# A fourth seven in the first column pair of w_down's second half, sevens loaded by rows, and tile 1's banks opened one column pair sooner

## The chip, the core and the metric

The kernel runs on one core of one Trainium2 chip. The time is device microseconds of one execution; three runs gave 1061.6, 1061.85 and 1062.74, the median is 1061.85 us. Nothing else runs on the chip.

The engines are named as in the profile: PE (TensorE; PEld is its weight load), DVE (VectorE), ACT (ScalarE), POOL (GpSimd) and SP, whose queue starts nearly all transfers.

## The reference, cut to what matters

One layer of a hybrid decoder in float32 for 256 positions of 2048 channels: an attention sub-layer, then a channel mixer. The change is in the mixer's last product:

```
h = rmsnorm(x, pre_ffn_g[l])
u = causal_dwconv(h @ w_up[l], conv_w[l], conv_b[l])
gate, val = jnp.split(u, 2, axis=-1)
y = (jax.nn.gelu(gate, approximate=True) * val) @ w_down[l]
x = x + rmsnorm(y, post_ffn_g[l])
```

`w_up` is 2048 x 11264, `w_down` is 5632 x 2048.

## The kernel before

**Three passes.** Each float32 operand is split into a high part (fp32r, a cast on ACT) and a low part (the rest, a subtraction on DVE), and a product is three matmuls: high by high, high by low, low by high. `split` (L286) and `w_split` (L107, its cast is L118 and its subtraction L121) do that; `products` (L973, matmul L975) issues the three. Weights come in units of 512 KB through five buffers `raw`, split into five pairs of buffers `whi` and `wlo`.

**The mixer in halves.** The 5632 rows of `w_down` are taken in two halves of 22 blocks of 128 rows. For each half the up-projection makes the 22 activation blocks `G` (positions are two tiles of 128, t = 0 and 1), and then `w_down` is applied to them in two column pairs, n = 0 and n = 2, of twice 512 columns. The first half leaves its sums in `y_sb`, the second adds to them. While the up-projection runs, DVE, ACT and POOL also make, for the first few pairs of blocks, four sums of quarters of `G` (L943 to L954), held split in `sums`.

**Fours and sevens.** A unit is two blocks of 128 rows and 512 columns. `four` (L1024) multiplies it plainly: 2 blocks by 2 tiles are 4 products, 12 matmuls, into two banks. A round is one `four` for each half of the column pair, 24 matmuls. `seven` (L988) does the work of one round, 2 blocks by 2 tiles by 2 column halves, with 7 products instead of 8 (21 matmuls, the Strassen-Winograd scheme): it takes sums of the weight blocks (four subtractions on DVE, L1002 to L1005, written in place into `raw`) and the sums of `G`. Three of its products are issued at once, on bank a (`w11`), b (`w21`) and e (`w22`); the other four, into banks d, f, c and g, come after the round's fours, from the function `others` that it returns. `SEVENS` lists in which rounds of a column pair a seven stands ahead of the fours. After the last seven `fold` (L1031) adds the four shared banks a, c, d and f into `y_sb`, in the second half with eight additions on DVE and a copy on ACT. At the end of a column pair `down` (L963) adds banks b, g, e and h to `y_sb` (L965), which frees them for the next pair; in the second half it also takes the squares (L967) and multiplies by the gain.

**Banks.** PSUM has eight banks here, four tagged `acc` and four tagged `att`, given out in turn: a new one waits until the oldest free one has been read for the last time.

**The last 512 columns.** In the second half the second pair (`tail`) does only the columns of n = 2. The last 512 columns are done after it: tile 0 in bank e, tile 1 in two banks `b1` of 256 columns each, so that half of tile 1 can be finished while PE does the other (L1140 on). `b1` is opened by a matmul with `start` (L1113) that only marks the banks as written, and then ACT copies tile 1's sums of the first half into them (L1114), so that the matmuls of `mm3` (L284) add to these.

**Order.** PE's order is the program's. DVE, ACT, POOL and SP are put in order by a scheduler when the program is built, except in a few stretches; the change is in scheduled ones. SP also brings back the residual, `x_end` (L1131, two loads of 1 MB), into the memory of `sums`, so it waits until the last seven is done.

Of the kernel before, what the change touches and what calls it, by code (L numbers as in the profile page):

```python
# [17 lines left out]
P = 128  # L18
# [6 lines left out]
NEG = -1e30  # L25
FHALF = 22
HOLD = 6
SEVENS = (((0, 1, 3, 4), (0, 1, 3, 4)), ((0, 2, 4), ()))
LOW = (14, 4, 4, 4)
ROOM = 112  # L30

# [2 lines left out]
def hybrid_layer(ctx: ExitStack, tc: tile.TileContext, x, pre_mix_g, w_in, b_forget, sinks,  # L34
# [3 lines left out]
    pe, act, dve, pool, sp = nc.tensor, nc.scalar, nc.vector, nc.gpsimd, nc.sync  # L38
    xf, of = x[0], out[0]
    w_in, w_out, w_up, w_down = w_in[0], w_out[0], w_up[0], w_down[0]  # L40
# [11 lines left out]
    def bank(tag="acc"):  # L52
        return ps.tile([P, 512], F32, tag=tag, bufs=4, name="bank_" + tag)
# [13 lines left out]
    UNIT = 1024  # L67
    WB = 5

    def w_load(src, a, c, pin=False):  # L70
        raw = wp.tile([P, UNIT], F32, tag="raw", bufs=5, name="raw")
        i = sp.dma_start(raw[:, :a * c].rearrange("p (a c) -> p a c", a=a), src)
        if pin:
            tc.keep_in_program_order(i)
        return raw, a, c
# [3 lines left out]
    def w_parts(n, keep=None, held=True):  # L79

        if keep and keep[0] is None:
            return keep[1]
        where, pre, nb = (keep[0], "h", keep[1]) if keep else (wp, "w", WB)
        hi = where.tile([P, UNIT], F32R, tag=pre + "hi", bufs=nb, name="whi")
        if where is not wp:
            lo = where.tile([P, UNIT], F32R, tag=pre + "lo", bufs=nb, name="wlo")
            return hi[:, :n], lo[:, :n]
        lo = where.tile([P, UNIT + 128], F32R, tag=pre + "lo", bufs=nb, name="wlo")
        at = 0
        if held:  # L90
            at = LOW[unit[0] % period[0]] * 4
            unit[0] += 1
        return hi[:, :n], lo[:, at:at + n]
# [35 lines left out]
    def w_rows(w, k0, a, c0, c):  # L129
        return w[k0 * P:(k0 + a) * P, c0:c0 + c].rearrange("(a p) c -> p a c", p=P)  # L130
# [18 lines left out]
    for i in range(2):  # L149
        cs = slice(i * 256, (i + 1) * 256)  # L150
# [135 lines left out]
    def split(hi, lo, src):  # L286
        act.copy(hi, src)  # L287
        dve.tensor_tensor(lo, src, hi.bitcast(F32), op=ALU.subtract)  # L288

    with tc.tile_pool(name="mixp", bufs=1) as mp:  # L290
# [3 lines left out]
        att = tc.tile_pool(name="att", bufs=1)  # L294
# [114 lines left out]
        halves = slice(0, 64), slice(64, 128)  # L409
# [192 lines left out]
        for p0, npair, cols in ((0, 3, 384), (3, 3, 384), (6, 2, 272)):  # L602
# [3 lines left out]
            for k0 in range(0, KT, per):  # L606
                na = min(per, KT - k0)
                hi, lo = w_unit(w_rows(w_in, k0, na, c0, cols), na, cols)
# [211 lines left out]
    with tc.tile_pool(name="ffn", bufs=1) as fp:  # L820
# [87 lines left out]
        for half in range(2):  # L908
# [70 lines left out]
            def parts_of(k, t):  # L979
                return G[k][:, t * P:(t + 1) * P], G[k][:, 256 + t * P:256 + (t + 1) * P]  # L980

            def split_512(dst, i, src):
                cs = slice(i * 512, i * 512 + 512)
                hi, lo = dst[0][:, cs], dst[1][:, cs]
                split(hi, lo, src)
                return hi, lo

            def seven(n, u, last, banks, opened):  # L988

                b, e, g, a, c, d, f = banks  # L990
                k = half * FHALF + u * 2
                left, right = [w_load(w_rows(w_down, k, 2, m * 512, 512), 2, 512)[0]
                               for m in (n, n + 1)]
                b11, b21, b12, b22 = (x[:, i * 512:i * 512 + 512] for x in (left, right)
                                      for i in range(2))
                s1, s2, s3, s4 = [(sums[:, u, i * P:i * P + P],
                                   sums[:, u, 512 + i * P:640 + i * P]) for i in range(4)]
                dst = w_parts(UNIT, held=False)
                w11 = split_512(dst, 0, b11)
                w22 = split_512(dst, 1, b22)  # L1000
                w21 = split_512(w_parts(UNIT, held=False), 0, b21)
                dve.tensor_tensor(b11, b12, b11, op=ALU.subtract)  # L1002
                dve.tensor_tensor(b12, b22, b12, op=ALU.subtract)
                dve.tensor_tensor(b22, b22, b11, op=ALU.subtract)
                dve.tensor_tensor(b21, b21, b22, op=ALU.subtract)  # L1005
                products(a, parts_of(u * 2, 0), *w11, opened, last)
                products(b, parts_of(u * 2 + 1, 0), *w21, opened)
                products(e, s4, *w22, opened)

                def others():  # L1010
                    dst = w_parts(UNIT, held=False)
                    t1 = split_512(dst, 0, b11)
                    t3 = split_512(dst, 1, b12)
                    dst = w_parts(UNIT, held=False)
                    t2 = split_512(dst, 0, b22)
                    t4 = split_512(dst, 1, b21)
                    products(d, s1, *t1, opened, last)
                    products(f, s3, *t3, opened, last)
                    products(c, s2, *t2, opened, last)
                    products(g, parts_of(u * 2 + 1, 1), *t4, opened)  # L1020

                return others
# [30 lines left out]
            for n in (0, 2):  # L1053
                opened = []
                tail = half and n
                at = SEVENS[half][n // 2]
                shared = [bank("att") for _ in range(4 if at else 0)]
                b, e, g = [bank() for _ in range(3)]
                h = None if tail else bank()
                for i in range(FHALF // 2 - len(at)):  # L1060
                    others = None
                    if i in at:
                        u = at.index(i)
                        others = seven(n, u, u == len(at) - 1, (b, e, g, *shared), opened)
                    four(n, len(at) + i, (b, g), opened)
                    if not tail:
                        four(n + 1, len(at) + i, (e, h), opened)
                    if others:
                        others()
                    if at and i == at[-1]:  # L1070
                        fold(n, *shared)
                    if i == max((0, *at)):
                        for args, kw in gains:
                            pool.tensor_tensor(*args, **kw)
                later_on = None if tail else lambda *args, **kw: gains.append((args, kw))
                for t, x in enumerate((b, g)):
                    down(t, n, x, later_on)
                if not tail:
                    for t, x in enumerate((e, h)):
                        down(t, n + 1, x, later_on)  # L1080
# [27 lines left out]
            q.dma_start(of[t * P:(t + 1) * P, cs], y_sb[:, t, cs])  # L1108

        held = []  # L1110
        b1 = [bank("att"), bank("att")]
        for x, cs in zip(b1, halves):
            pe.matmul(x[:, cs], G[0][:, 0:P], G[0][:, 0:256], start=True, stop=False)  # L1113
            act.copy(x[:, cs], y_sb[:, 1, 1536:2048][:, cs])  # L1114
        for u in range(len(at), FHALF // 2):
            hi, lo = w_unit(w_rows(w_down, FHALF + u * 2, 2, 1536, 512), 2, 512,
                            keep=(None, [rest[:, c:c + 2, :].rearrange("p a c -> p (a c)")
# [10 lines left out]
                    held.append(args)  # L1128
        x_sb = main.tile([P, 2, D], F32, tag="x", name="x_end")
        for t in range(2):  # L1130
            sp.dma_start(x_sb[:, t, :], x_dram[t * P:(t + 1) * P, :])  # L1131
        ctx.enter_context(tc.manual_schedule(
            engines={mybir.EngineType.Activation, mybir.EngineType.DVE, mybir.EngineType.Pool,
                     mybir.EngineType.SP}))
# [47 lines left out]
```

## Time and profile before

| | us |
|---|---|
| median of three runs | 1061.85 |
| the profiled execution | 1063.41 |
| its span, first to last instruction | 1061.7 |
| PE busy | 1050.2 (99%) |
| DVE busy | 803.8 (76%) |
| ACT busy | 634.0 (60%) |
| POOL busy | 252.1 (24%) |
| granted clock of PE, mean | 0.999 |

The first half's `w_down` lies between about 577 and 692 us, the second half's first column pair between 932.8 and 990.6, its second up to 1020.7, the last 512 columns up to 1053.7. A profiled row gives the start and the length of an instruction, in brackets how long its engine had been idle and what ended that. Rows with "x2" hold two instructions in a row. A matmul's length is from its start to the modelled end of its output, and the next one starts before that, so the price of one is the distance of two starts.

### The profile page before, as it was taken

The page shows a single profiled execution, that of the slowest core. Times are in us where ns is not written, and L with a number is a line of the kernel's source. Part 1 is how long each engine was busy: PE and PEld are TensorE (multiplying, and loading weights), DVE is VectorE, ACT ScalarE, POOL GpSimd, SP SyncE. Part 2 cuts the span into 40 slices and gives each one's busy share as a digit, 9 for nine tenths or more (in the row PEclk, how much of TensorE's full clock was granted, in tenths as well). Part 3 has the DMA queues.
Part 4 walks back from the last instruction along what each step waited for, and adds up shares of the span by engine and source line. Part 5 has one row for each costly group of instructions (what it writes and reads, how often), then busy time and mean ns, then how long its engine had stood idle before and what let it go on. Part 6 is the DMA issues. An engine that isn't in the chain of part 4 may idle for free.

```text
span 1061.7 us, 16409 instructions
## 1 busy us (share of the span) xinstructions
PE 1050.2 (99%) x5941; PEld 914.6 (86%) x5941; DVE 803.8 (76%) x1330; ACT 634.0 (60%) x1119; POOL 252.1 (24%) x278
## 2 busy tenths in 40 slices
PE   9999999999999999999999999999999999999996
PEld 7889988888889888888888888888888888888886
DVE  5989877876468787777768888868786777787653
ACT  6767766677557666655556555556565556555450
POOL 4253235441122433312111000013321212100210
PEclk9999999999999999999999999999999999999999
DMA  8645665555875766666664666866576656557742
GB/s 279 204 120 169 179 204 189 180 158 160 297 237 178 226 201 197 200 189 201 185 195 139 209 207 196 251 194 192 179 211 192 193 181 199 175 162 267 270 154 80
DMA packets 165550, 207.10 MB, mean 195 GB/s; under 512 B 6844, under 2 KB 131036, under 8 KB 164444
## 3 DMA queue, kind: packets, MB, share of 16 engines
q1 hardware_dynamic: 165148, 205.65, 61.9%
q8 instruction: 47, 0.77, 0.3%
q10 hardware_dynamic: 320, 0.40, 0.1%
q14 instruction: 35, 0.29, 0.1%
HBM read 201.68 MB, written 4.21 MB: 194 GB/s over the span
## 4 chain that ended last, share of the span: by engine, by line
PE 90%; DVE 4%; DMA 2%; issue 2%; ACT 1%; POOL 0%; SPq 0%; DVEq 0%; POOLq 0%; ACTq 0%
PE bank_acc L262 21%; PE bank_att L262 15%; PE bank_acc L975 13%; PE bank_acc L284 13%; PE bank_acc L269 11%; PE bank_att L269 8%; DMA raw<-in_w_down_dram 2%; PE bank_att L975 2%; DVE wlo L121 1%; PE bank_att L450 1%; PE bank_att L485 1%; PE bank_att L494 1%; DVE wlo L288 1%; PE bank_att L225 1%; PE bank_acc L881 1%
## 5 line engine op out<-in xcount | busy, mean ns | idle before, releaser
L121 DVE TENSOR_TENSOR wlo<-raw,whi 128x1024 fp32r<-128x1024 f32 (+3 forms) x335 | 408.7, 1233 | 140.4 <-ACT whi L118 133.5
L118 ACT CAST whi<-raw 128x1024 fp32r<-128x1024 f32 (+3 forms) x334 | 340.8, 1035 | 196.7 <-issue 90.7
L262 PE MATMUL bank_acc<-hT,whi 128*128 128x512 f32 x1024 | 245.6, 392 | 0.0
L262 PEld LDWEIGHTS bank_acc<-hT,whi 128*128 128x128 f32 x1024 | 188.2, 188 | 37.1
L857 POOL TENSOR_TENSOR u<-u,rowf 128x256 f32<-128x256 f32 x88 | 94.5, 1095 | 447.3 <-DVE u L856 444.3
L975 PE MATMUL bank_acc<-whi,G 128*128 128x512 f32 x520 | 167.6, 389 | 0.1
L262 PE MATMUL bank_att<-hT,whi 128*128 128x512 f32 x704 | 165.7, 390 | 0.0
L262 PEld LDWEIGHTS bank_att<-hT,whi 128*128 128x128 f32 x704 | 130.6, 188 | 26.2
L269 PEld LDWEIGHTS bank_acc<-hT,wlo 128*128 128x128 f32 x1024 | 123.5, 188 | 3.2
L269 PE MATMUL bank_acc<-hT,wlo 128*128 128x256 f32 x1024 | 125.8, 278 | 0.0
L975 PEld LDWEIGHTS bank_acc<-whi,G 128*128 128x128 f32 x520 | 97.6, 188 | 20.3 <-DVE y_sb L965 0.5
L975 PE MATMUL bank_acc<-wlo,G 128*128 128x512 f32 x260 | 101.2, 389 | 0.0
L269 PEld LDWEIGHTS bank_att<-hT,wlo 128*128 128x128 f32 x704 | 83.6, 188 | 1.9
L269 PE MATMUL bank_att<-hT,wlo 128*128 128x256 f32 x704 | 83.9, 277 | 0.0
L284 PE MATMUL bank_acc<-whi,oT 128*128 128x512 f32 (+1 forms) x272 | 81.8, 379 | 0.0
L287 ACT CAST whi<-raw 128x512 fp32r<-128x512 f32 x77 | 44.4, 621 | 27.2 <-DMA raw<-in_w_down_dram 14.5
L288 DVE TENSOR_TENSOR wlo<-raw,whi 128x512 fp32r<-128x512 f32 x77 | 52.7, 727 | 9.9 <-ACT whi L287 9.8
L284 PEld LDWEIGHTS bank_acc<-whi,oT 128*128 128x128 f32 x272 | 50.2, 188 | 9.3
L975 PEld LDWEIGHTS bank_acc<-wlo,G 128*128 128x128 f32 x260 | 48.8, 188 | 9.8
L284 PE MATMUL bank_acc<-wlo,oT 128*128 128x512 f32 (+1 forms) x136 | 51.2, 377 | 0.0
L284 PE MATMUL bank_acc<-whi,hT 128*128 128x384 f32 (+1 forms) x192 | 46.9, 323 | 0.0
L859 ACT ACTIVATE yg<-u,cw 128x256 f32<-128x256 f32 x44 | 26.5, 603 | 33.7 <-POOL u L857 33.7
(250 smaller groups left out, 1284.4 us busy)
## 6 DMA issues: line engine op xcount, KB each, us to landing
raw<-in_w_up_dram SPq DMA_DIRECT2D x176, 512.0 KB, 4.5
raw<-in_w_down_dram SPq DMA_DIRECT2D x88, 512.0 KB, 4.9
raw<-in_w_in_dram SPq DMA_DIRECT2D x51, 512.0 KB, 4.9
raw<-in_w_out_dram SPq DMA_DIRECT2D x32, 512.0 KB, 4.7
raw<-in_w_in_dram SPq DMA_DIRECT2D x16, 384.0 KB, 3.3
cb<-c_dram SPq DMA_DIRECT2D x8, 256.0 KB, 4.2
x_sb<-in_x_dram SPq DMA_DIRECT2D x2, 1024.0 KB, 6.0
x_dram<-x_sb SPq DMA_DIRECT2D x2, 1024.0 KB, 5.9
```

The source lines that it names most:

```text
L118: i1 = act.copy(hi[:, cs], raw[:, cs])
L121: i2 = dve.tensor_tensor(lo[:, cs], raw[:, cs], hi[:, cs].bitcast(F32), op=ALU.subtract)
L225: pe.matmul(b, hi[:, a, m * P:(m + 1) * P], hT[:, kt, 0:512], start=(kt == 0), stop=(kt == KT - 1))
L262: pe.matmul(b, hi[:, a, m * P:(m + 1) * P], hT[:, kt, 0:512], start=(kt == 0), stop=(last == (0, kt)))
L269: pe.matmul(b[:, 256:512], lo[:, a, m * P:(m + 1) * P], hT[:, u * 4 + a, 0:256], start=False, stop=(last == (1, u * 4 + a)))
L284: pe.matmul(b, a, r[:, cols], start=(first and i == 0), stop=(last and i == 2))
L287: act.copy(hi, src)
L288: dve.tensor_tensor(lo, src, hi.bitcast(F32), op=ALU.subtract)
L450: pe.matmul(sb[e][:, cs], a[r, t * P:(t + 1) * P], b[r, 0:nk], start=(n == 0), stop=(n == 2))
L857: pool.tensor_tensor(u[:, 2:258], u[:, 2:258], rowf, op=ALU.mult)
L859: act.activation(y, u[:, 2:258], AF.Identity, bias=cw[:, 3, ch:ch + 1], scale=cw[:, 2, ch:ch + 1])
L975: pe.matmul(b, x, r, start=b not in opened and not i, stop=closes and i == 2)
```

## The change

Three things are changed.

1. `SEVENS` gives the second half's first column pair sevens in rounds 0, 1, 3 and 4 instead of 0, 2 and 4. The pair has 7 rounds of fours then instead of 8. `most` becomes 4, so the up-projection of that half makes a fourth set of sums.
2. A seven's weights, a square of two blocks by two column halves, are loaded as two rows of 1024 columns (`top`, `low`) instead of as two columns of two blocks (`left`, `right`), and split with `split_into` in four pieces (512, 1024, 1024 and 1024 wide) instead of seven of 512.
3. The two matmuls and two copies that open `b1` move from behind the tail pair to behind its first round.

A fourth edit, which keeps the loads of `x_end` in program order, is made only if `at` is not empty there; it is empty here, so nothing follows from it.

```diff
-SEVENS = (((0, 1, 3, 4), (0, 1, 3, 4)), ((0, 2, 4), ()))
+SEVENS = (((0, 1, 3, 4), (0, 1, 3, 4)), ((0, 1, 3, 4), ()))
...
-            def split_512(dst, i, src):
-                cs = slice(i * 512, i * 512 + 512)
-                hi, lo = dst[0][:, cs], dst[1][:, cs]
-                split(hi, lo, src)
-                return hi, lo
+            def split_into(dst, src, n):
+                hi, lo = (x[:, :n * 512] for x in dst)
+                split(hi, lo, src[:, :n * 512])
+                return [(hi[:, i:i + 512], lo[:, i:i + 512]) for i in range(0, n * 512, 512)]
...
-                left, right = [w_load(w_rows(w_down, k, 2, m * 512, 512), 2, 512)[0]
-                               for m in (n, n + 1)]
-                b11, b21, b12, b22 = (x[:, i * 512:i * 512 + 512] for x in (left, right)
-                                      for i in range(2))
+                top, low = [w_load(w_rows(w_down, k + i, 1, n * 512, 1024), 1, 1024)[0]
+                            for i in range(2)]
+                b11, b12, b21, b22 = (x[:, i:i + 512] for x in (top, low) for i in (0, 512))
...
-                dst = w_parts(UNIT, held=False)
-                w11 = split_512(dst, 0, b11)
-                w22 = split_512(dst, 1, b22)
-                w21 = split_512(w_parts(UNIT, held=False), 0, b21)
+                (w11,) = split_into(w_parts(UNIT, held=False), top, 1)
+                w21, w22 = split_into(w_parts(UNIT, held=False), low, 2)
...
-                    dst = w_parts(UNIT, held=False)
-                    t1 = split_512(dst, 0, b11)
-                    t3 = split_512(dst, 1, b12)
-                    dst = w_parts(UNIT, held=False)
-                    t2 = split_512(dst, 0, b22)
-                    t4 = split_512(dst, 1, b21)
+                    t1, t3 = split_into(w_parts(UNIT, held=False), top, 2)
+                    t4, t2 = split_into(w_parts(UNIT, held=False), low, 2)
...
                     if i == max((0, *at)):
                         for args, kw in gains:
                             pool.tensor_tensor(*args, **kw)
+                    if tail and i == (at[-1] + 4 if at else 0):
+                        b1 = [bank("att"), bank("att")]
+                        for x, cs in zip(b1, halves):
+                            pe.matmul(x[:, cs], G[0][:, 0:P], G[0][:, 0:256], start=True,
+                                      stop=False)
+                            act.copy(x[:, cs], y_sb[:, 1, 1536:2048][:, cs])
...
         held = []
-        b1 = [bank("att"), bank("att")]
-        for x, cs in zip(b1, halves):
-            pe.matmul(x[:, cs], G[0][:, 0:P], G[0][:, 0:256], start=True, stop=False)
-            act.copy(x[:, cs], y_sb[:, 1, 1536:2048][:, cs])
...
-            sp.dma_start(x_sb[:, t, :], x_dram[t * P:(t + 1) * P, :])
+            i = sp.dma_start(x_sb[:, t, :], x_dram[t * P:(t + 1) * P, :])
+            if at:
+                tc.keep_in_program_order(i)
```

The change takes lines away and puts others in, so the line numbers of what lies behind differ: the fold's additions L1044 to L1051 are L1036 to L1043 after it, the opening L1113 is L1070; L965 and L121 keep theirs.

Where it moves instructions, the built programs show it. On DVE, at the end of the second half's first column pair, the order before is this. The banks `acc` 9938, 9940, 9939 and 9941 are b, g, e and h; L121 is the split of a unit, L1049 to L1051 the end of the fold.

```order
L121 TENSOR_TENSOR wlo_10378<-raw_10375,whi_10377 128x1024
L1049 TENSOR_TENSOR y_sb_3952<-y_sb_3952,s_10275 128x512
L1050 TENSOR_TENSOR s_10275<-bank_att_9936,s_10275 128x512
L121 TENSOR_TENSOR wlo_10407<-raw_10404,whi_10406 128x1024
L1051 TENSOR_TENSOR y_sb_3952<-y_sb_3952,s_10275 128x512
L121 TENSOR_TENSOR wlo_10429<-raw_10426,whi_10428 128x1024
L121 TENSOR_TENSOR wlo_10447<-raw_10444,whi_10446 128x1024
L965 TENSOR_TENSOR y_sb_3952<-bank_acc_9938,y_sb_3952 128x512
L965 TENSOR_TENSOR y_sb_3952<-bank_acc_9940,y_sb_3952 128x512
L121 TENSOR_TENSOR wlo_10465<-raw_10462,whi_10464 128x1024
L965 TENSOR_TENSOR y_sb_3952<-bank_acc_9939,y_sb_3952 128x512
L965 TENSOR_TENSOR y_sb_3952<-bank_acc_9941,y_sb_3952 128x512
```

On DVE at the same place after the change, where banks b, g, e and h are 9897, 9899, 9898 and 9900:

```order
L121 TENSOR_TENSOR wlo_10385<-raw_10382,whi_10384 128x1024
L1041 TENSOR_TENSOR y_sb_3952<-y_sb_3952,s_10261 128x512
L1042 TENSOR_TENSOR s_10261<-bank_att_9895,s_10261 128x512
L121 TENSOR_TENSOR wlo_10403<-raw_10400,whi_10402 128x1024
L1043 TENSOR_TENSOR y_sb_3952<-y_sb_3952,s_10261 128x512
L965 TENSOR_TENSOR y_sb_3952<-bank_acc_9897,y_sb_3952 128x512
L965 TENSOR_TENSOR y_sb_3952<-bank_acc_9899,y_sb_3952 128x512
L121 TENSOR_TENSOR wlo_10421<-raw_10418,whi_10420 128x1024
L965 TENSOR_TENSOR y_sb_3952<-bank_acc_9898,y_sb_3952 128x512
L965 TENSOR_TENSOR y_sb_3952<-bank_acc_9900,y_sb_3952 128x512
```

Before, two splits of units stood between the end of the fold and the four L965; now the first two L965 follow the fold at once, and one split, that of the eighth unit after the last seven, stands ahead of the third. On PE, the third of these banks (e, read by the third L965) is the one that the next column pair's second product is given.

On PE, before, the opening of `b1` (banks `att` 10612 and 10613) stands between the tail pair's last products and the last 512 columns; `acc` 10402 is bank e of tile 0:

```order
L975 MATMUL bank_acc_10403<-wlo_10591,G21_7488 128x512
L975 MATMUL bank_acc_10403<-whi_10590,G21_7488 128x512
L1113 MATMUL bank_att_10612<-G0_7467 128x256
L1113 MATMUL bank_att_10613<-G0_7467 128x256
L975 MATMUL bank_acc_10402<-whi_10620,G0_7467 128x512
L975 MATMUL bank_acc_10402<-wlo_10621,G0_7467 128x512
L975 MATMUL bank_acc_10402<-whi_10620,G0_7467 128x512
L284 MATMUL bank_att_10612<-whi_10620,G0_7467 128x256
```

On PE after the change, the opening (banks 10376 and 10377) stands between the tail pair's first and second unit:

```order
L975 MATMUL bank_acc_10353<-wlo_10357,G1_7420 128x512
L975 MATMUL bank_acc_10353<-whi_10356,G1_7420 128x512
L1070 MATMUL bank_att_10376<-G0_7419 128x256
L1070 MATMUL bank_att_10377<-G0_7419 128x256
L975 MATMUL bank_acc_10351<-whi_10384,G2_7421 128x512
L975 MATMUL bank_acc_10351<-wlo_10385,G2_7421 128x512
```

The pair of opening matmuls has moved ten units ahead; the matmul that first adds to `b1` (L284) stands where it stood.

## The prediction

> **What bounds the kernel now.** I read the page first, then the chain of waits from 940 us on, then what TensorE (PE) waited for, then the timeline at the places that the change touches.
>
> ```profile
> span 1061.7 us, 16409 instructions
> PE 1050.2 (99%) x5941; PEld 914.6 (86%) x5941; DVE 803.8 (76%) x1330; ACT 634.0 (60%) x1119; POOL 252.1 (24%) x278
> ```
>
> PE is busy for 1050.2 of 1061.7 us, so the number of products sets the time, and what else there is to gain lies in the few places where PE stands still. The chain from 940 us on (start, length, what) shows one of them:
>
> ```profile
> 971.71 2.04 PE bank_att L975 x9
> 973.75 46.93 PE bank_acc L975 x207
> 1020.68 0.02 issue
> 1020.70 0.84 ACT whi L118
> ...
> 1023.30 0.28 ACT bank_att L1114
> 1023.58 0.04 issue
> 1023.62 0.62 PE bank_att L284 x3
> ...
> 1024.94 0.71 PE bank_att L284 x6
> ```
>
> From 973.75 us on, 207 matmuls follow each other without a break: 46.93 / 207 = 0.2267 us each, which is the price of a 512-wide matmul here (its own row says 0.39, because neighbours overlap). Then the chain leaves PE for ScalarE (ACT) until 1023.62. These are all the waits of PE for such work (total us, times, longest), and its weight loads (PEld) tell the same:
>
> ```profile
> PE bank_att L284 <- ACT bank_att L1114: 1.4, 2, 1.1
> PEld bank_att L284 <- ACT bank_att L1114: 2.0, 2, 1.5
> PEld bank_acc L975 <- DVE y_sb L965: 0.5, 1, 0.5
> ```
>
> The first two lines are the opening of tile 1's banks. The third is a column pair's start that waits for VectorE (DVE) to empty a bank. No row names a weight split or a weight load: the feeding of the sevens is hidden, and a cheaper feeding gains nothing by itself.
>
> **The change part by part.**
>
> *The fourth seven.* The pair had 3 sevens of 21 matmuls and 8 rounds of 24 (63 + 192 = 255); it gets 4 and 7 (84 + 168 = 252). Three matmuls at 0.2267 us go: -0.68 us. They lie in a stretch without a break, so all of it counts. Bounds: none worth the name.
>
> It also needs one more set of sums. DVE and ACT rows of these, and GpSimd's (POOL) four small operations before them:
>
> ```profile
> L948 POOL TENSOR_TENSOR s<-yv x7: 2319/2322/2381, 365.1 to 763.6; 128x128 f32<-128x128 f32 x7
> L287 ACT CAST sums<-s x7: 621/622/625, 369.0 to 767.4; 128x512 fp32r<-128x512 f32 x7
> L288 DVE TENSOR_TENSOR sums<-s,sums x7: 691/693/693, 369.7 to 768.1; 128x512 fp32r<-128x512 f32 x7
> ```
>
> Seven such sets were made beside the up-projection, four of them in the first half, and PE's waits above name none. The eighth is put at nothing; were its cover gone, 0.62 + 0.69 = 1.3 us would show.
>
> *Tile 1's banks.* PE's starts around the opening:
>
> ```profile
> 1021.21 0.39 PE L975 MATMUL bank_acc<-whi,G 128*128 128x512 f32 x1
> 1022.70 0.38 PE L284 MATMUL bank_att<-whi,G 128*128 128x256 f32 x1 [1.10 <-ACT bank_att L1114]
> ...
> 1023.62 0.39 PE L284 MATMUL bank_att<-whi,G 128*128 128x256 f32 x1 [0.31 <-ACT bank_att L1114]
> ...
> 1024.08 0.40 PE L975 MATMUL bank_acc<-whi,G 128*128 128x512 f32 x1
> ```
>
> From 1021.21 to 1024.08 are 2.87 us, for one 512-wide matmul (0.23) and six 256-wide ones (0.71, the chain's last row above): 1.93 us are lost. ACT filled the banks behind a weight cast and the squares of the pair just finished. With the opening after the pair's first unit, the copies have ten units of 2.72 us (12 x 0.2267) to run in. On PE the two opening matmuls cost the same there and wait for banks that the first steps of the fold have long given back; on ACT the copies stand between weight casts that run several units ahead, and hold up nobody. What is late next at the old place? Nothing that a row names: no PE wait is for a split. So -1.93 us; the least that the rows allow is the 1.4 us put down as idle.
>
> *Sevens by rows.* Each of the now 12 sevens makes four splits instead of seven, with the same elements. Two 512-wide splits, queued, take 1.20 us (966.47 to 967.67 below), a 1024-wide one 1.14 (976.50 to 977.64), so DVE saves some 0.2 us a seven, off the path. Whether longer rows arrive sooner is bounded by the issue rows (median us to landing):
>
> ```profile
> raw<-in_w_up_dram SPq DMA_DIRECT2D x176, 512.0 KB, 4.5
> raw<-in_w_down_dram SPq DMA_DIRECT2D x88, 512.0 KB, 4.9
> ```
>
> w_up comes in pieces of 1 KB, w_down of 2 KB, and the longer pieces are not the quicker: nothing for the step to 4 KB. The first half holds one wait that this could move, the third PE wait above, worth 0.33 us (worked below): bounds -0.33 and +0.33, and I take 0.
>
> *The wait that the change adds.* After the last seven DVE has the fold (L1044 to L1051), then four adds L965 that empty the pair's banks. Number the units of four after the last seven 1, 2, 3 and so on: the pair used to end after unit 6, now it ends after unit 4, 24 matmuls or 5.44 us sooner, while the fold is as long as before. The next pair's third bank is free only after the third L965, and in the new order the splits of units 4 to 8 stand ahead of that. On DVE, ACT and SP's queue, before:
>
> ```profile
> 966.47 1.29 DVE L288 TENSOR_TENSOR wlo<-raw,whi 128x512 fp32r<-128x512 f32 x2
> 967.67 0.68 DVE L1044 TENSOR_TENSOR y_sb<-bank_att,y_sb 128x512 f32<-128x512 f32 x1
> 968.27 1.28 DVE L288 TENSOR_TENSOR wlo<-raw,whi 128x512 fp32r<-128x512 f32 x2
> ...
> 973.97 0.68 DVE L1045 TENSOR_TENSOR s<-bank_att,s 128x512 f32<-128x512 f32 x1
> 976.50 1.23 DVE L121 TENSOR_TENSOR wlo<-raw,whi 128x1024 fp32r<-128x1024 f32 x1 [1.84 <-ACT whi L118]
> 977.64 0.68 DVE L1046 TENSOR_TENSOR y_sb<-y_sb,s 128x512 f32<-128x512 f32 x1
> ...
> 984.17 0.69 DVE L1051 TENSOR_TENSOR y_sb<-y_sb,s 128x512 f32<-128x512 f32 x1
> 984.77 1.22 DVE L121 TENSOR_TENSOR wlo<-raw,whi 128x1024 fp32r<-128x1024 f32 x1
> ...
> 990.29 1.28 DVE L965 TENSOR_TENSOR y_sb<-bank_acc,y_sb 128x512 f32<-128x512 f32 x2
> ```
>
> ```profile
> 975.41 1.05 ACT L118 CAST whi<-raw 128x1024 fp32r<-128x1024 f32 x1 [2.62 <-DMA raw<-in_w_down_dram]
> ...
> 983.32 1.06 ACT L118 CAST whi<-raw 128x1024 fp32r<-128x1024 f32 x1 [2.35 <-DMA raw<-in_w_down_dram]
> ```
>
> ```profile
> 968.99 3.24 SPq L72 DMA_DIRECT2D raw<-in_w_down_dram  x4
> ```
>
> ```profile
> 990.36 0.62 PE L975 MATMUL bank_acc<-whi,G 128*128 128x512 f32 x2
> ```
>
> The second of the last two matmuls, 990.36 + 0.23 = 990.59, opens the next pair; its third bank is wanted 0.68 us later, and the third L965 had ended by 990.98: just in time. On the same clock the new boundary is at 990.59 - 5.44 = 985.15, and the third bank is wanted at 985.83. DVE, from the start of unit 4's split (976.50) without idling: 7.67 to L1051, 0.60 for it, two L965 at 0.60, unit 8's split 1.14, the third L965 0.69, together 11.30: it would end at 987.80. What a late third L965 costs after that is shown by the first half's boundary, where this wait stands already (PE, its weight load, DVE):
>
> ```profile
> 637.10 0.95 PE L975 MATMUL bank_acc<-whi,G 128*128 128x512 f32 x2
> ```
>
> ```profile
> 637.55 0.19 PEld L975 LDWEIGHTS bank_acc<-whi,G 128*128 128x128 f32 x1 [0.49 <-DVE y_sb L965]
> ```
>
> ```profile
> 636.81 1.28 DVE L965 TENSOR_TENSOR y_sb<-bank_acc,y_sb 128x512 f32<-128x512 f32 x2
> ```
>
> The L965 ends at 637.49, the weights load from 637.55, the matmul starts at 637.10 + 0.95 - 0.39 = 637.66 instead of 637.33: a stall of 0.33 us, and 0.17 us from the end of the add to the matmul. So here PE would restart at 987.97 instead of 985.83: a stall of 2.14 us, if unit 4's split starts where it did.
>
> That start hung on a load: SP issued unit 4's at 968.99, when the third of the last seven's four splits gave back its buffer, and the cast waited for it until 975.41 (6.4 us). By rows, the first of two 1024-wide splits gives back its tile at 966.47 + 1.23 = 967.70, 1.29 us sooner. If the load takes as long, unit 4 starts at 975.21 and the stall is 0.85 us. If the load were no matter, the split would follow L1045 at once, at 974.57, and the stall is 2.14 - 1.93 = 0.21 us. Unit 8's load, which comes behind the first half of x_end on SP's queue now as before, had its cast done at 984.38; in the middle case its split is due at 975.21 + 7.67 + 0.60 + 1.20 = 984.68, so it does not hold. I take 0.85, since its load time is the one measured at this place; both ends stay in the range.
>
> [...]
>
> *Sum.* -0.68 - 1.93 + 0.85 = -1.76 us. The profiled execution took 1063.41 us (1.7 around its span), to become 1061.65; the median of the runs is 1061.85, to become 1060.1 us. A measurement of this kernel can tell about 0.2%, 2.1 us, from no change, so this is a gain just under that.
>
> **The rivals.**
>
> *The loads are early enough.* With sevens in consecutive rounds DVE may run further ahead of PE, and the row tiles come back sooner still. Then 0.21 us is left, or less: 1061.85 - 2.40 = 1059.45 us. For it: no PE wait in the whole page of waits is for a load of w_down. Against: at this very place the casts at 975.41 and 983.32 waited for loads. [...]
>
> *The loads are as late as before.* Four sevens in five rounds ask for the same bytes in less time, and unit 4 starts no sooner: stall 2.14, sum -0.47, 1061.4 us. For it: the first half, which has that order of sevens, is the one with a stall. Against: the buffer does come back earlier.
>
> *Slower: the second product of every seven waits for a whole row.* The half-empty second split becomes 1024 wide, cast and subtraction, and two products now hang on the second load. In the first half (DVE, then PE):
>
> ```profile
> 584.33 2.49 DVE L288 TENSOR_TENSOR wlo<-raw,whi 128x512 fp32r<-128x512 f32 x4
> ```
>
> ```profile
> 588.37 0.39 PE L975 MATMUL bank_acc<-whi,G 128*128 128x512 f32 x1
> ```
>
> The last of these four splits ends at 586.82 and the product's second matmul uses it at 588.60: a lead of 1.78 us. The wider split adds about 1.0 us between load and use (1.05 instead of 0.62 for the cast, 1.14 instead of 0.60 for the subtraction). It decides once that lead is gone: at 0.6 us lost in each of 12 sevens, +7.2, the time is 1061.85 - 1.76 + 7.2 = 1067.3. Against: 0.8 us are left here, and no PE wait names a split.
>
> **How the numbers follow.** Forecast 0.45 (1060.1); loads early enough 0.28 (1059.45); loads late 0.22 (1061.4); whole rows waited for 0.05 (1067.3). The range takes in the first three with the 0.33 us of the first half's wait downwards (1059.45 - 0.33 - 0.21 = 1058.9, with no stall at all) and a little above the late case: 1058.9 to 1061.6. Faster by over 0.2% means under 1059.7: the early case nearly whole and the lower edge of the forecast's, 0.27 + 0.10 = 0.37. Slower by over 0.2% is the last case, 0.04 of its 0.05. Within: 0.59.
>
> **What would show it.** In the profile after, PE waits no longer name the bank copy; the pair's boundary has a PEld wait on L965 of about a microsecond, the third L965 right behind a split; the cast of unit 4 waits for its load. A boundary without a wait is the early case, one of 2 us the late one. A PE wait on a seven's split, or a median outside 1058.9 to 1061.6, would make me wrong; so would a gap still standing at the last pair's start.

## The result, and the profile after

The kernel after took 1058.88 us (median of 9 runs, 1058.49 to 1059.99), the kernel before beside it 1061.60 (9 runs, 1061.40 to 1062.74): 2.72 us less, ratio 0.9976, 95% interval 0.9966 to 0.9985. Forecast were 1.76 us less and 1060.1 us, with a range from 1058.9: the sign was right and the forecast gain 1 us too small. The median lies at the range's lower edge (0.02 us under it as written); taken from the 1061.85 us that the prediction started from, 2.72 us less is 1059.13, inside it.

The page after, and all waits of PE in it (total us, times, longest):

```profile
span 1057.2 us, 16352 instructions
PE 1047.3 (99%) x5938; PEld 912.8 (86%) x5938; DVE 808.9 (77%) x1304; ACT 632.8 (60%) x1089; POOL 256.6 (24%) x282
```

```profile
PE bank_acc L173 <- DVE junk L168: 1.3, 1, 1.3
PE bank_att L494 <- DVE pl L288: 0.5, 1, 0.5
```

Three matmuls fewer (5938), and no wait for a bank copy or for an add L965 is left; both rows belong to the first part of the kernel. The span is 4.5 us shorter, more than the medians allow. Where that comes from is read off the chains of waits at the same four places: inside the first up-projection, at the second up-projection's start, at the second w_down's start, and at the end of the last 512 columns. Before, then after (start, length, what):

```profile
563.06 7.28 PE bank_acc L262 x32
...
692.27 3.63 PE bank_att L262 x16
...
933.63 6.80 PE bank_acc L975 x30
...
1036.90 8.20 PE bank_acc L975 x36
```

```profile
561.50 7.29 PE bank_acc L262 x32
...
690.33 3.63 PE bank_att L262 x16
...
931.69 6.80 PE bank_acc L975 x30
...
976.57 14.28 PE bank_acc L975 x63
991.09 27.91 PE bank_acc L975 x123
1018.99 0.71 PE bank_att L284 x6
...
1032.37 8.20 PE bank_acc L975 x36
```

The first row differs by 1.56 us, ahead of all changed work: that is how this one execution of before began, and no gain of the change. PE waited 0.6 us longer there for a piece of x, and its next four 512-wide matmuls took 2.05 us (from 7.27 us on) where those after took 1.23 (from 6.62 on); the trace's record of the granted clock begins at 10.64 us there and at 6.74 after. Why those four took longer is not shown. From the first to the second row it is 129.21 against 128.83 (-0.38, most of it a wait of 0.33 us in the first half, see "Rows alone"), to the third 241.36 in both, to the fourth 103.27 against 100.68 (-2.59). The chain no longer leaves PE: 63 matmuls, the opening between 990.85 and 991.09, 123 matmuls, and the first product of tile 1 at the old place without a gap. -2.59 is -0.68 and -1.93 (-2.61) with no new stall at all.

The pair boundary, where the prediction had put +0.85 us. DVE after, then PE:

```profile
985.67 1.28 DVE L965 TENSOR_TENSOR y_sb<-bank_acc,y_sb 128x512 f32<-128x512 f32 x2
986.87 1.22 DVE L121 TENSOR_TENSOR wlo<-raw,whi 128x1024 fp32r<-128x1024 f32 x1
988.00 1.28 DVE L965 TENSOR_TENSOR y_sb<-bank_acc,y_sb 128x512 f32<-128x512 f32 x2
```

```profile
987.74 0.61 PE L975 MATMUL bank_acc<-whi,G 128*128 128x512 f32 x2
988.20 0.39 PE L975 MATMUL bank_acc<-wlo,G 128*128 128x512 f32 x1
988.42 0.61 PE L975 MATMUL bank_acc<-whi,G 128*128 128x512 f32 x2
```

The second matmul of the first PE row, at 987.97, is the first of the last pair; the second one of the third row, at 988.65, opens that pair's second bank. The third add runs from 988.00 to 988.68. PE did not wait for it. It needs the banks that the first two adds had emptied by 986.36 and 986.95. The built program says so outright: the last pair's first product waits for the first add and its second product for the second add, since its bank is that of g; the bank of e, which the third add empties, goes to the last 512 columns. So the section on the change has this wrong where it gives the second product the bank of e.

And unit 4's cast, which before waited 2.62 us for its load (ACT after; it is the second row):

```profile
974.57 1.05 ACT L118 CAST whi<-raw 128x1024 fp32r<-128x1024 f32 x1 [1.67 <-PE bank_acc L975]
975.93 1.06 ACT L118 CAST whi<-raw 128x1024 fp32r<-128x1024 f32 x1 [0.30 <-PE bank_att L975]
```

It waits for PE to give back a split tile, as its predecessor does, and not for its load.

### The profile page after: what moved, and what is told of

It is laid out like the page before. It is cut to its first block, busy times and chain, and to the rows that moved or that the text cites. A ratio compares the mean times of both kernels' runs of the same rounds, so it can differ in the third digit from the quotient of the medians.

```text
span 1057.2 us, 16352 instructions
## 1 busy us (share of the span) xinstructions
PE 1047.3 (99%) x5938; PEld 912.8 (86%) x5938; DVE 808.9 (77%) x1304; ACT 632.8 (60%) x1089; POOL 256.6 (24%) x282
## 4 chain that ended last, share of the span: by engine, by line
PE 96%; DVE 1%; issue 1%; DMA 1%; ACT 0%; SPq 0%; POOL 0%; DVEq 0%; POOLq 0%; ACTq 0%
PE bank_acc L262 21%; PE bank_acc L975 17%; PE bank_att L262 15%; PE bank_acc L284 13%; PE bank_acc L269 11%; PE bank_att L269 8%; PE bank_att L975 3%; PE bank_att L450 1%; PE bank_att L485 1%; PE bank_att L494 1%; PE bank_acc L881 1%; PE bank_acc L225 1%; PE bank_att L284 1%; DMA x_in<-in_x_dram 1%; PE bank_att L225 1%
## 5 line engine op out<-in xcount | busy, mean ns | idle before, releaser
L121 DVE TENSOR_TENSOR wlo<-raw,whi 128x1024 fp32r<-128x1024 f32 (+3 forms) x333 | 407.5, 1236 | 131.6 <-ACT whi L118 124.0
L975 PE MATMUL bank_acc<-whi,G 128*128 128x512 f32 x508 | 164.1, 389 | 0.0
L975 PEld LDWEIGHTS bank_acc<-whi,G 128*128 128x128 f32 x508 | 95.4, 188 | 19.4
L975 PE MATMUL bank_acc<-wlo,G 128*128 128x512 f32 x254 | 98.9, 389 | 0.0
L284 PE MATMUL bank_acc<-whi,oT 128*128 128x512 f32 (+1 forms) x272 | 81.7, 379 | 0.0
L287 ACT CAST whi<-raw 128x1024 fp32r<-128x1024 f32 (+1 forms) x48 | 44.3, 943 | 28.2 <-PE bank_acc L975 16.9
L284 PEld LDWEIGHTS bank_acc<-whi,oT 128*128 128x128 f32 x272 | 50.2, 188 | 9.3
L288 DVE TENSOR_TENSOR wlo<-raw,whi 128x1024 fp32r<-128x1024 f32 (+1 forms) x48 | 51.8, 1103 | 6.9 <-ACT whi L287 6.6
L975 PEld LDWEIGHTS bank_acc<-wlo,G 128*128 128x128 f32 x254 | 47.7, 188 | 9.5
L284 PE MATMUL bank_acc<-wlo,oT 128*128 128x512 f32 (+1 forms) x136 | 51.2, 377 | 0.0
L284 PE MATMUL bank_acc<-whi,hT 128*128 128x384 f32 (+1 forms) x192 | 46.9, 323 | 0.0
```

The source lines that it names most:

```text
L121: i2 = dve.tensor_tensor(lo[:, cs], raw[:, cs], hi[:, cs].bitcast(F32), op=ALU.subtract)
L284: pe.matmul(b, a, r[:, cols], start=(first and i == 0), stop=(last and i == 2))
L975: pe.matmul(b, x, r, start=b not in opened and not i, stop=closes and i == 2)
```

## The experiments

Theory 1, formed from the trace after: the parts add up (-0.68 and -1.93), and TensorE waits at the boundary only for the two banks that the last pair opens, whose adds have 1.4 us in hand. Theory 2 is the prediction's: the third add is waited for. All differences below are medians against runs of the kernel before on the same chip.

| kernel | us less (-) or more than before | ratio, 95% interval |
|---|---|---|
| fourth seven alone | -0.54 | 0.9996 (0.9987 to 1.0005) |
| opening alone | -2.04 | 0.9981 (0.9972 to 0.9990) |
| rows alone | -0.10 | 0.9999 (0.9990 to 1.0008) |
| after, loads by columns | -2.52 | 0.9978 (0.9970 to 0.9987) |
| after, opening at the old place | -0.71 | 0.9993 (0.9984 to 1.0001) |
| after, adds written in another order | -2.70 | 0.9974 (0.9963 to 0.9984) |
| after, sevens in rounds 0 to 3 | -2.66 | 0.9973 (0.9963 to 0.9984) |
| after, last seven in round 5 | -2.36 | 0.9977 (0.9967 to 0.9986) |
| after, one operation ahead of the adds | -1.44 | 0.9986 (0.9978 to 0.9995) |
| after, two | +2.31 | 1.0024 (1.0015 to 1.0034) |
| after, three | +3.93 | 1.0036 (1.0023 to 1.0049) |

**The fourth seven alone** (before, with the table's one line):

```
-SEVENS = (((0, 1, 3, 4), (0, 1, 3, 4)), ((0, 2, 4), ()))
+SEVENS = (((0, 1, 3, 4), (0, 1, 3, 4)), ((0, 1, 3, 4), ()))
```

> The kernel before with the fourth seven alone; columns loaded as before, tile 1's banks opened at the old place. Theory 1 (the next pair needs only the banks of the first two adds L965, which have over a microsecond in hand): three matmuls fewer and nothing else, -0.68 us, no wait of TensorE at the pair boundary of the second half. Theory 2 (the prediction's: the third add L965 is waited for): with the columns unit 4's load is late, 2.14 us of stall, +1.46 us in all. Both: the gap at the opening of tile 1's banks stays near 2 us, and the first half keeps its 0.33 us wait if that wait comes from the loads by columns.

Measured -0.54: near theory 1, far from +1.46. Its profiled execution took longer than most (1062.46 us against the median of 1060.87) and had its loads late, and so shows what late loads cost. ACT's casts, DVE, then PE:

```profile
976.03 1.05 ACT L118 CAST whi<-raw 128x1024 fp32r<-128x1024 f32 x1 [1.89 <-DMA raw<-in_w_down_dram]
979.37 1.05 ACT L118 CAST whi<-raw 128x1024 fp32r<-128x1024 f32 x1 [2.29 <-DMA raw<-in_w_down_dram]
```

```profile
988.73 1.28 DVE L965 TENSOR_TENSOR y_sb<-bank_acc,y_sb 128x512 f32<-128x512 f32 x2
...
991.06 1.28 DVE L965 TENSOR_TENSOR y_sb<-bank_acc,y_sb 128x512 f32<-128x512 f32 x2
```

```profile
988.62 0.39 PE L975 MATMUL bank_acc<-whi,G 128*128 128x512 f32 x1
989.55 0.47 PE L975 MATMUL bank_acc<-whi,G 128*128 128x512 f32 x1 [0.55 <-DVE y_sb L965]
989.86 0.40 PE L975 MATMUL bank_acc<-wlo,G 128*128 128x512 f32 x1
990.09 0.62 PE L975 MATMUL bank_acc<-whi,G 128*128 128x512 f32 x2
```

The adds start 57.00 us after w_down's start, 2.2 us later than in the kernel after. PE begins the last pair 0.14 us after the first add's end (989.41) instead of at 988.85, opens the second bank at 990.32, and pays 0.79 us in all (0.71 and 0.08 between matmuls). That is about half of the 1.59 us over the median; the rest lies ahead of w_down, which starts at 931.72 us here and at 930.85 in the kernel after. The third add has not begun by then: it ends at 991.74, and waiting for it would have cost 2.4 us. So even the late case, which the prediction priced at 2.14 us, costs 0.8.

**The opening alone** (the four lines at the opening moved into the loop, as in the change, at `i == 0` of the last pair; nothing else):

> The kernel before with only the opening and filling of tile 1's banks moved behind the last pair's first unit. Theory 1 and the prediction alike: the gap of 1.93 us goes and nothing takes its place, -1.93 us. Rival: the copies delay the casts behind them on ScalarE at the new place, or the cast and squares at the old place still hold TensorE: -1.4 us or less, with a new wait of TensorE or of its weight loads near the new place.

Measured -2.04; the second w_down takes 119.01 us in its profile instead of 120.93 (first L975 to the last matmul's end). At the new place PE goes on without a gap, and ACT makes the two copies behind a cast, done by 993.1, 26 us before tile 1's first product:

```profile
991.03 0.39 PE L975 MATMUL bank_acc<-whi,G 128*128 128x512 f32 x1
991.26 0.40 PE L1078 MATMUL bank_att<-G 128*128 128x256 f32 x2
991.49 0.40 PE L975 MATMUL bank_acc<-whi,G 128*128 128x512 f32 x1
```

```profile
991.46 1.06 ACT L118 CAST whi<-raw 128x1024 fp32r<-128x1024 f32 x1 [0.29 <-PE bank_acc L975]
992.42 0.67 ACT L1080 COPY bank_att<-y_sb 128x256 f32<-128x256 f32 x2
```

That is three quarters of the whole gain. The two profiles differ there by the 1.93 us of the prediction to a hundredth (120.93 and 119.01 us), and no new wait of PE or its weight loads stands at the new place: the rival is out.

**Rows alone** (before, with the new `split_into` and `seven`):

> The kernel before with only the sevens' weights loaded and split by rows. Theory 1: buffers come back sooner, unit 4 of the first half starts about 1.9 us sooner, and the 0.33 us wait at the first half's pair boundary goes: -0.33 us. Rival (that wait came and went by chance of the execution): 0, and the wait can be there or not with either way of loading. The profiled execution tells: cast of the unit after the last seven waiting for its load by about 3 us or not.

Measured -0.10, no difference. The 0.33 us wait of the first half is gone in its profile, but it is gone as well in the profiles of the two kernels above, which load by columns: the rival holds, that wait came by chance of the one execution of before. The first half's w_down takes 114.62 us there and 114.24 in every other profile, by columns or by rows.

**The kernel after with columns** (`split_512` and the old `seven` back):

> The kernel after with the sevens' weights loaded and split by columns again (fourth seven and early opening stay). Theory 1: -0.68 - 1.93 = -2.61 us against the kernel before, with the 0.33 us wait of the first half back; the adds of the second half's first pair come later than in the kernel after by some 1.3 us, which the 1.4 us in hand still cover, so at most a few tenths of a stall. Theory 2: unit 4's load is late as before and the third add is waited for, stall 2.14 us, -0.47 us.

Measured -2.52, and no stall at the boundary or in the first half: theory 1, though two of its details failed. The first half's wait did not come back, and the adds come 0.04 us later than in the kernel after (54.86 us after w_down's start against 54.82), not 1.3. The second w_down takes 118.33 us in both profiles. Loading by rows brings nothing that these runs can tell, and costs nothing.

**The kernel after with the opening at the old place**:

> The kernel after with tile 1's banks opened and filled at the old place again (the fourth seven and the loads by rows stay). If the parts add up: 1.93 us slower than the kernel after, -0.68 us against the kernel before, with the gap of 1.9 us back at the opening. If the two changes share a cost (the ScalarE work at the pair boundary), the boundary shows a stall, as it did in the profiled execution of the fourth seven alone (0.79 us), or the gap at the opening has another length.

Measured -0.71. The boundary has no stall, and the old gap is back as it was (PE; compare 1021.21 to 1024.08 before: 2.87 us there, 1018.45 to 1021.32 here, 2.87 too):

```profile
1018.45 0.39 PE L975 MATMUL bank_acc<-whi,G 128*128 128x512 f32 x1
1019.94 0.38 PE L284 MATMUL bank_att<-whi,G 128*128 128x256 f32 x1 [1.10 <-ACT bank_att L1106]
...
1020.86 0.38 PE L284 MATMUL bank_att<-whi,G 128*128 128x256 f32 x1 [0.30 <-ACT bank_att L1106]
...
1021.32 0.40 PE L975 MATMUL bank_acc<-whi,G 128*128 128x512 f32 x1
```

-0.71 for seven and rows, -2.04 for the opening: -2.75 together, -2.72 measured. The parts add up. The intervals of these medians are about 0.9 us to either side, so the profiles say it more sharply: the second w_down takes 120.93 us before, 120.25 here (-0.68), 119.01 with the opening alone (-1.92) and 118.33 after (-2.60).

**The adds in another order.**

```
+if not tail and half:
+    for t, x in enumerate((e, h)):
+        down(t, n + 1, x, later_on)
 for t, x in enumerate((b, g)):
     down(t, n, x, later_on)
-if not tail:
+if not tail and not half:
```

> The kernel after, but in the second half's first pair the adds L965 empty the banks of its second column (e, h) first and those of its first column (b, g) after: the banks that the last pair opens at once are now emptied third and fourth. In the kernel after the third add ends at 988.69 and TensorE enters the last pair at 987.97. Theory 1 (TensorE waits for the two banks that it opens, whichever add empties them): with 0.17 us from an add's end to the matmul the pair starts at 988.86, a stall of 0.89 us, 0.9 us slower than the kernel after (-1.8 against the kernel before where the kernel after is at -2.7). Theory 2 (all adds up to the third, whichever bank it empties): nothing changes, the time of the kernel after.

Measured -2.70, the kernel after. This tells nothing: the scheduler put the adds in the old order, b and g first, so that DVE and PE run the same instructions in the same order as in the kernel after. It is a repeat.

**Sevens in rounds 0 to 3** (`(0, 1, 2, 3)` in all three pairs):

> The kernel after with all three pairs' sevens in rounds 0, 1, 2 and 3 instead of 0, 1, 3 and 4: the fold starts one round (two units, 5.4 us) sooner before each boundary. If the boundaries are free of waits as the trace of the kernel after shows, nothing is to be gained there: 0 against the kernel after. Rival: four sevens in a row ask for splits and loads faster than VectorE and the queue give them (a seven needs four splits and four subtractions, about 7 us of VectorE, beside 4.8 us of matmuls and its two units' 5.4): new waits of TensorE on a split, up to a few us slower.

Measured -2.66, the time of the kernel after: nothing is left to win at the boundaries, and four sevens in a row are fed in time (no wait of PE in its profile is for a split or a load of w_down).

**The last seven in round 5** (`(0, 1, 3, 5)` in the second half):

> The kernel after with the second half's sevens in rounds 0, 1, 3 and 5: the fold starts two units (5.44 us) nearer to the pair boundary. On VectorE the fold's eight operations, the splits between and the adds keep their order but have 5.44 us less; some 1.4 us were in hand and two splits fewer (2.3 us) stand ahead of the adds. Theory 1: stall up to 5.44 - 1.44 - 2.3 = 1.7 us, and less by what else moves; somewhere from 0 to 1.7 us slower than the kernel after. Theory 2: 1.9 us more than that (3.6 us), since the third add is two operations and a split later than the first.

Measured -2.36, 0.36 more than the kernel after; 0.33 us in the profile (118.66 us for the second w_down). The operations did not keep their order, as had been expected: the scheduler put the first three adds between the fold's last ones. DVE, and PE's weight loads:

```profile
986.98 0.68 DVE L965 TENSOR_TENSOR y_sb<-bank_acc,y_sb 128x512 f32<-128x512 f32 x1
...
988.18 0.68 DVE L965 TENSOR_TENSOR y_sb<-bank_acc,y_sb 128x512 f32<-128x512 f32 x1
988.78 0.68 DVE L1042 TENSOR_TENSOR s<-bank_att,s 128x512 f32<-128x512 f32 x1
989.38 0.68 DVE L965 TENSOR_TENSOR y_sb<-bank_acc,y_sb 128x512 f32<-128x512 f32 x1
```

```profile
988.91 0.19 PEld L975 LDWEIGHTS bank_acc<-whi,G 128*128 128x128 f32 x1 [0.46 <-DVE y_sb L965]
```

The weights for the last pair's second bank are loaded 0.05 us after the second add's end (988.86), while the third add ends at 990.06: theory 2 is out. In the built program that pair's second tile lies here in the bank of e, which the second add empties in this order, and in the kernel after in the bank of g: it gets the bank that comes free second, whatever its name.

**One, two and three operations ahead of the adds** (k = 1, 2, 3):

```
+if half and not tail:
+    for _ in range(k):
+        dve.scalar_tensor_tensor(y_sb[:, :, 0:512], y_sb[:, :, 512:1024], 0.0,
+                                 y_sb[:, :, 0:512], op0=ALU.mult, op1=ALU.add)
```

> The kernel after with one extra operation of VectorE (128 x 2 x 512, zero times the pair's second column added to its first) between the fold and the four adds L965; one weight split slips ahead of the adds too. The first add then starts 1.14 + 1.14 us later, at 987.95 on the clock of the kernel after, and ends at 988.63; with 0.17 us more the last pair would start at 988.80 instead of 987.97. Theory 1 (1.44 us in hand, then every microsecond counts): 0.83 us slower than the kernel after, TensorE standing at the first matmul of the last pair. Theory 2 (third add): it comes 1.15 us later than in the kernel after, so 1.35 us at the second bank. Where the profiled execution has its loads late, as the one of the fourth seven alone, the stall is that much longer. A stall this short should leave the granted clock at 1.0: the gaps of 1.26 and 0.71 us seen so far did.

Measured -1.44, that is 1.28 us slower than the kernel after (taken at its -2.72, as in the next two). PE:

```profile
987.97 0.39 PE L975 MATMUL bank_acc<-whi,G 128*128 128x512 f32 x1
989.37 0.47 PE L975 MATMUL bank_acc<-whi,G 128*128 128x512 f32 x1 [1.01 <-DVE y_sb L965]
```

The first add started 57.46 us after w_down's start instead of 54.82, 2.64 us later and not 2.28, and the stall is 1.25 us (1.17 and 0.08 between matmuls): 1.39 us were in hand, as theory 1 says (1.44). It stands at the pair's first matmul, not at the second bank.

> The kernel after with two extra operations of VectorE (128 x 2 x 512, each adding zero times the pair's second column to its first) between the fold and the four adds L965; by the program's order two weight splits also slip ahead of the adds. The first add then starts some 4.6 us later, at about 990.3 on the clock of the kernel after, instead of 985.67. Theory 1: the 1.44 us in hand are used up first, stall about 3.1 to 3.3 us, so 3.2 us slower than the kernel after. Theory 2 (third add, 0.2 us late already): the third add comes about 3.5 us later than in the kernel after, stall about 3.5 to 3.7 us and more for the first two banks than for the third. The place of the wait tells: by theory 1 TensorE stands at its first matmul of the last pair, with the first add as releaser.

> The same with three such operations; two weight splits slip ahead of the adds. The first add starts 5 x 1.14 = 5.7 us later, at 991.37, and the last pair at 992.22 instead of 987.97: a stall of 4.25 us. With two such operations the stall measured 4.75 us and the granted clock then fell to 0.5 for 3.41 us, which cost 1.6 us more. Theory K (a standstill of some 4 us halves the clock for the next 3.4 us): 4.25 + 1.6 to 1.7 = 5.9 us slower than the kernel after. Rival (the fall of the clock was chance): 4.25 us.

Measured 5.0 and 6.7 us slower than the kernel after, where 3.2 and 5.9 were expected. The place is theory 1's: in both, PE's only new wait is for the first add. With two, the profiled execution stood 4.7 us, and there a load was late once more (a cast after the last seven waited 2.15 us for it); at 1065.61 us it lies 1.7 us over this kernel's median, so it is not the typical case. But the stall is not the whole price, and the rest is told in the last section.

## Why the prediction was right or wrong

**The sum, -1.76: too small, by its boundary term.** Without the +0.85 the prediction's own terms make -2.61, and -2.72 was measured. A boundary without a wait was its sign of the early case, which it gave 0.28; but that case, too, still charged 0.21 us to the third add. That the range reached far enough is in part luck: its lower edge took in 0.33 us of a wait in the first half that was not the change's to move.

**The seven, -0.68: right.** -0.71 with rows, -0.54 with columns; the interval of neither is narrow enough to tell the two apart, and the profiles give -0.68 (120.93 to 120.25 us). The eighth set of sums cost nothing: the stretch from the second up-projection's start to w_down's is 241.36 us before and after.

**The opening, -1.93: right.** -2.04 alone. The floor of 1.4 us, the idle time that the waits named, was too low: the gap in PE's starts was the price, not the wait put down to ACT.

**Rows, 0: right,** and the 0.33 us that I kept in the range for the first half's wait was not the change's to move. It stands in one profile only, that of before.

**The boundary, +0.85: wrong, measured 0.** Two steps failed. The first is the one that decides: with it alone put right nothing is left to wait for, with the second alone put right 0.21 us of stall remain. It is "The next pair's third bank is free only after the third L965", taken as wanted 0.68 us into the last pair; the section on the change says the same of the pair's second product. The first half's boundary does work like that, since there a seven and the four behind it open b, e and g within three microseconds, and from it I took the price. But the last pair opens only b and g at once; its third bank, e's product, is wanted not before 1018.1, in the last 512 columns. 0.68 us after the boundary its second bank is wanted, the old bank of g, which the second add had emptied 1.7 us earlier. In the profile of before the third add happened to end 0.29 us ahead of that moment (990.98 and 991.27), and I read a coincidence as "just in time".

The second step is the load, taken to be as long as the 6.4 us of the profile of before. In the profile after, unit 4's split begins as the early rival has it (DVE):

```profile
977.40 1.22 DVE L121 TENSOR_TENSOR wlo<-raw,whi 128x1024 fp32r<-128x1024 f32 x1
```

The prediction's clock, on which the last seven ends at 973.75, stands 2.82 us behind that of the profile after (976.57). On it unit 4's split was due at 974.57 and started at 977.40 - 2.82 = 974.58; the third L965 was due to end at 987.80 - 1.93 = 985.87 and ended at 988.68 - 2.82 = 985.86. DVE's rows summed to a hundredth of a microsecond; what was wrong is who waits for them. The loads by rows are not the reason that unit 4 came in time: with columns its split starts at 977.37, where it starts at 977.40 in the kernel after. Why that load was late in the profiles of before and of the fourth seven alone stays open.

The loads can still be late, as that profile shows, and then the price is 0.8 us and not 2.14. In the kernel after, too, they are not early throughout: the page has 4.8 us as the median of these loads, which SP issues (4.9 before), and the cast behind unit 4's (978.05) waited 1.06 us for one.

**The slower rival: out.** The first half's w_down takes 114.24 us, from its first L975 to the next up-projection, with rows as with columns, and no wait of PE in the profile after names a split in w_down, so no seven waits for its wider second split.

## What to carry to other kernels

Before a late operation is charged to an engine, name the instruction that waits for it and the buffer that it wants first at that very place; another place with the same code around it may want a third buffer at once where this one wants two. Work that fills accumulators ahead of a chain belongs a stage earlier, where its engine has time: moving two copies was worth three times as much as three matmuls fewer (2.04 us alone against 0.71). A single profile's short wait (0.33 us here) is not yet a property of the kernel, and its span can be off by more than half of what the change is worth (1.56 us at the start here, of 2.72).

## What the runs showed of the hardware

Two standstills of TensorE cost more than their length: 4.75 us in the profile of the kernel with two operations cost 6.35, and 4.52 us in that of the kernel with three (987.87 to 992.62, less 0.23 for a matmul) cost 6.75. The kernel with two, then the one with three, in stretches of 3.41 us, cut so that the granted clock (PEclk) changes only between two rows:

```profile
986.91:990.33 3.42, 1.60 (x8) 1.00 0.74 237
990.33:993.74 3.41, 0.72 (x3) 1.00 0.93 325
993.74:997.15 3.41, 3.41 (x9) 0.50 0.77 290
997.15:1000.56 3.41, 3.41 (x17) 1.00 0.08 32
```

```profile
986.91:990.32 3.41, 1.35 (x6) 1.00 1.05 375
990.33:993.74 3.41, 1.12 (x3) 0.50 0.99 396
993.74:997.15 3.41, 3.41 (x10) 0.50 0.24 92
997.15:1000.56 3.41, 3.41 (x18) 1.00 0.00 0
```

The columns are stretch, us, PE's busy time (matmuls), granted clock, DMA share, GB/s. At the clock of 0.50 a 512-wide matmul starts every 0.43 us (with two operations, 994.24 and 994.67) instead of 0.2267. With two operations the stall was 4.75 us (4.67 and 0.08); the clock fell at 993.74 us, 5.2 us after the end of the last matmul ahead of the stall (988.52) and 0.7 us after PE had gone on (993.02), and was back at 1.00 from 997.15 on, 3.41 us later: 6.35 us lost from w_down's start to its last matmul. With three, the clock fell during the stall, at 990.33 us, 2.1 us after the end of the last matmul ahead of it (988.26), and was back from 997.15 on, 6.82 us later: 6.75 us lost. The idle times of 1.10 and 0.31 us at the opening in the profile of before, and the stall of 1.25 us of the kernel with one operation, left it at 1.00.

The clock fell once more after the end of PE's work: in the profile of the kernel after at 1051.21 us, 2.0 us after the end of the last matmul (1049.18), and in the profile of before at 1058.53, 4.8 us after it (1053.72). The kernel after:

```profile
1047.80:1051.21 3.41, 1.38 (x12) 1.00 0.23 87
1051.21:1054.63 3.42, 0.00 (x0) 0.50 0.73 263
```

So in these four places it fell 2.0 to 5.2 us after a last matmul. What sets that time is not shown.
